# Seven block products for eight in three quarters of a feed-forward matrix

## The chip, the core and the metric

The kernel runs on one core of one Trainium2 chip. A core has five engines with a queue each: TensorE (PE) multiplies matrices, VectorE (DVE) and ScalarE (ACT) work element by element, GpSimd (POOL) here only issues DMAs, and SyncE (SP) issues the DMAs that load weights. Each engine takes its instructions in order; engines wait for each other through semaphores. TensorE reads SBUF and writes PSUM, which has eight banks of 128 x 512 float32; VectorE and ScalarE read both. Sixteen DMA engines serve all queues.

The metric is the time of one execution on the device, in microseconds (us), as the median of several runs.

## The reference

A hybrid encoder block over 256 tokens of width 2048 in float32: gated linear attention beside a Hyena convolution, merged, projected, added to the input and normalised; then a feed-forward part with width 8192. The change is in that last part:

```
    ff = jnp.square(jax.nn.relu(h @ w_ff1[l])) @ w_ff2[l]
    h = _layernorm(DEEPNORM_ALPHA * h + ff, ln2_g[l], ln2_b[l])
```

`h` is 256 x 2048, `w_ff1` 2048 x 8192, `w_ff2` 8192 x 2048.

## The kernel before

**Precision.** Each float32 operand is held as two parts: `hi`, rounded by a copy into TensorE's fast format on ScalarE (line 85), and `lo`, the rest, a subtraction on VectorE (line 86). A product of two operands is then hi x hi + hi x lo + lo x hi. A weight block is 128 x 2048 float32 (1 MB). `fetch` (line 93) loads one into one of three `raw` buffers from SP's queue and splits it in two halves of 1024 columns, each into one of three `whi` and three `wlo` buffers (`weight_half`, line 107).

**First matrix.** A block gives 128 of the 8192 channels for all 256 tokens. `channel_products` (line 140) runs, for each of 16 slices of the input, one matmul of 512 columns (hi weight against hi and lo activation side by side, line 146) and one of 256 (lo weight against hi activation, line 150). `channel_sum` (line 155) adds the two column halves of the result: ScalarE copies one, VectorE adds the other. `channel_pair` (line 161) does two blocks; `ff1` (line 1073) then squares the positive part on VectorE (line 1078) and splits the result into hi and lo.

**Second matrix.** `token_products` (line 194) takes a block that holds four slices of 512 columns: for each slice and each of two token blocks three matmuls of 512 columns (lines 205 to 207), 24 a block. `token_group` (line 209) runs four blocks into one PSUM bank for each token block, and `add_ff` (line 1089) adds the finished 128 x 512 sums to `z1`, the residual, on VectorE.

**Order.** The 8192 channels are done in four quarters of 2048: 16 blocks of the first matrix (`ff1(q)`) and 16 of the second (`ff2(q)`). Lines 1107 to 1117 run ff1(0), ff1(1), ff2(0), ff1(2), ff2(1), ff1(3), ff2(2), ff2(3). Within an engine's queue a scheduler orders instructions from their place in the program and an estimate of when their inputs are ready; `keep_in_program_order` fixes an instruction's place among the others that are fixed, `high_priority` moves it ahead, and `issue_after` ties it behind another instruction.

**Around it.** Before the first quarter, the first layer norm turns `z1` into `hT`, the normalised activations with channels on partitions, by TensorE transposes (line 1017), ScalarE copies and VectorE subtractions (line 86); `begin_three` (line 1038) starts three blocks during that. Four additions of the norm's bias rows to `z1` (line 1084) are tied behind VectorE's square of the blocks 2 to 5 (line 1083). `load_rows` (line 910) loads the second norm's scale and bias rows, from ScalarE's queue, after ff1(0). The last four blocks of the second matrix are held in SBUF (`resident`, line 918), so that the last column group can be finished token block by token block before the second layer norm.

Of the kernel before, what the change touches and what calls it, by code (L numbers as in the profile page):

```python
# [16 lines left out]
P = 128  # L17
# [12 lines left out]
W_OUT_END = 177  # L30
OPENING = 5
# [11 lines left out]
def block_kernel(  # L43
# [117 lines left out]
    def channel_pair(act, name, dst=None, scale=1.0, begun=None):  # L161
        if dst is None:
            dst = base.tile([P, 2, L], F32, tag="sum", name=f"{name}_s")
        for c in range(2):
            if begun:
                ps, parts, n = begun.pop(0)
                finish_block(ps, act, parts, n)
            else:
                ps = channel_psum(f"{name}_{c}")
                parts = next_block()  # L170
                for h in range(2):
                    channel_products(ps, act, parts[h], range(8 * h, 8 * h + 8))
            channel_sum(dst[:, c], ps, f"{name}_l{c}", scale)
            pump()
        return dst
# [742 lines left out]
    def resident(slots):  # L918
        parts = []
        for hi, lo in slots:  # L920
# [4 lines left out]
            for h in range(2):  # L925
                cs = slice(h * 1024, (h + 1) * 1024)
                split_hi_lo(hi[:, cs], lo[:, cs], raw[:, cs])
            parts.append([(hi[:, 0:1024], lo[:, 0:1024]), (hi[:, 1024:], lo[:, 1024:])])
        return parts

# [43 lines left out]
    for i, t in ((0, turn_b), (1, turn_i)):  # L974
        raw = ep.tile([P, 4, P], F32, tag="aff", bufs=1, name=f"turn{i}")
# [19 lines left out]
    stop_at[0] = nblk  # L995
# [40 lines left out]
    fts = {}  # L1036

# [35 lines left out]
    def ff1(qi):  # L1073
        begun = begin_three() if qi == 0 else []
        f = act_tile(ep, "f", f"f{qi}") if qi % 2 == 0 else act_tile(base, "xT", f"f{qi}")
        for c2 in range(8):
            r = channel_pair(hT, f"f{qi}_{c2}", begun=begun)
            sq = nc.vector.scalar_tensor_tensor(r, r, 0.0, r, op0=ALU.max, op1=ALU.mult)
            s = slice(2 * c2, 2 * c2 + 2)
            split_hi_lo(f[:, s, 0], f[:, s, 1], r)  # L1080
            if qi == 0 and 2 <= c2 < 6:
# [3 lines left out]
        fts[qi] = f  # L1085
# [3 lines left out]
    def add_ff(ps, tb, at, n, qi, last=False):  # L1089
        zc = z1[:, tb, at:at + n]  # L1090
        if qi == 0:
            nc.vector.scalar_tensor_tensor(zc, zc, ALPHA, ps, op0=ALU.mult, op1=ALU.add)
        else:
            nc.vector.tensor_tensor(zc, zc, ps, op=ALU.add)
        if qi == QT - 1:
            for i in range(n // 256):
                nc.vector.bn_stats(st2[:, tb, at // 256 + i, :], zc[:, i * 256:(i + 1) * 256])
            if not last:
                nc.vector.tensor_tensor(zc, zc, rows2[:, 0, at:at + n], op=ALU.mult)

    def ff2(qi, groups=4):
        for g in range(groups):
            pss = token_group(fts[qi], f"w2_{qi}{g}")
            for tb in range(NT):
                add_ff(pss[tb], tb, g * 512, 512, qi)
# [12 lines left out]
    minus = ep.tile([P, P], F32, tag="minus", name="minus")  # L1118
    nc.vector.tensor_scalar(minus, ident, -1.0, None, op0=ALU.mult)
    unit = ep.tile([P, P], F32R, tag="unit", name="unit")  # L1120
    nc.scalar.copy(unit, ident)
    zg = tuple(ep.tile([P, D], F32R, tag=t, name=f"{t}_z") for t in ("xh", "xl"))
    for at in (0, 768):
        split_hi_lo(zg[0][:, at:at + 768], zg[1][:, at:at + 768], z1[:, 1, at:at + 768])

    def affine(tb, at, n, rs, nb):
        zc = z1[:, tb, at:at + n]
        t = ep.tile([P, 512], F32, tag="aff", bufs=1, name=f"aff{tb}_{at}")[:, 0:n]
# [7 lines left out]
    token_products([ps], fts[3], parts, [0], 0)  # L1136
    pss = [psum_main(f"w2_33_1{ch}") for ch in range(2)]
    add_ff(ps, 0, 1536, 512, 3)
# [4 lines left out]
    column_products([None, pss], fts[3], parts, [1], 0)  # L1143
    CENTRED = ((0, 512), (512, 512), (1024, 256), (1280, 256))
    po = {}
    for at, n in CENTRED[:3]:
        po[at] = psum_side(f"lo{at}")
        for part in zg:
            tc.keep_in_program_order(MM(po[at], unit, part[:, at:at + 512], start=(part is zg[0]), stop=False))
    po[1280] = po[1024][:, 256:]  # L1150
    add_ff(pss[0][:, 0:256], 1, 1536, 256, 3, last=True)
    late = z1[:, 1, 1536:2048]
    with tc.high_priority(), tc.issue_after(done.ins):
        add_ff(pss[1][:, 0:256], 1, 1792, 256, 3, last=True)
# [21 lines left out]
def _layout(a):  # L1176
# [24 lines left out]
    for i in range(NCH // 2):  # L1201
# [4 lines left out]
    f2q = [tok(w2[D * i:D * (i + 1)]) for i in range(QT)]  # L1206
# [4 lines left out]
        + [f1q[0], f1q[1], f2q[0], f1q[2], f2q[1], f1q[3], f2q[2], f2q[3]], axis=0)  # L1211
# [100 lines left out]
```

## Time and profile before

| | |
|---|---|
| median of 3 runs | 1825.76 us (1825.61 to 1826.41) |
| the profiled execution, first to last instruction (span) | 1826.2 us |
| mean granted TensorE clock in it | 1.000 |
| matmuls of the second matrix, start of the first and of the last | 1288.9 and 1815.7 us after the start |
| HBM read, written | 369.28 MB, 16.25 MB |

Of the profiled execution no other time is known than its span, which lies within the three runs. How to read a profile line: times are in us from the span's start, durations in us unless marked ns; `L205` is a line of the kernel; `w<-whi,f` says that tile `w` is written from `whi` and `f`; `x2` counts instructions; what stands in brackets is the engine's idle time before it and what ended that. PE is TensorE's matmuls, PEld its weight loads, which overlap them. Matmuls are pipelined, so one that is shown with 0.39 us can be followed by the next much sooner.

### The profile page before, as it was taken

How to read it: one execution, taken by the hardware profiler on the slowest of the kernel's cores; microseconds unless marked ns; L12 is line 12 of the kernel's file. 1: busy time of each engine (PE TensorE's matmuls, PEld its weight loads, DVE VectorE, ACT ScalarE, POOL GpSimd, SP SyncE). 2: the span in 40 equal slices, each digit the busy share in tenths (PEclk: the TensorE clock that was granted, in tenths of full speed). 3: DMA queues.
4: the chain of work that ended last, by engine and by line, in shares of the span. 5: the costliest groups of instructions: out<-in, count | busy, mean ns of one | idle time of the engine just before them, and what ended most of it. 6: DMA issues, size and time to landing. Idle time of an engine off the chain costs nothing.

```text
span 1826.2 us, 22887 instructions
## 1 busy us (share of the span) xinstructions
PE 1817.0 (99%) x8931; PEld 1533.8 (84%) x8931; DVE 1286.8 (70%) x1587; ACT 924.1 (51%) x1207; POOL 80.4 (4%) x121
## 2 busy tenths in 40 slices
PE   9999999999999999999999999999999999999998
PEld 7888888888888888888888889888888888888887
DVE  6789887875689899898755567666545655565467
ACT  6678668865444444444544445444434443443332
POOL 1011110000111101020000000000000000000000
PEclk9999999999999999999999999999999999999999
DMA  8668765345788979796544763545554555555453
GB/s 326 222 257 293 253 220 204 141 162 210 235 281 255 320 249 274 259 281 230 215 186 185 288 252 137 210 185 188 193 196 186 193 195 187 195 195 187 188 197 123
DMA packets 65452, 399.55 MB, mean 219 GB/s; under 512 B 8280, under 2 KB 10856, under 8 KB 24640
## 3 DMA queue, kind: packets, MB, share of 16 engines
q1 hardware_dynamic: 47808, 336.61, 49.1%
q0 software_dynamic: 10480, 41.81, 9.9%
q10 hardware_dynamic: 7056, 19.67, 3.0%
q8 instruction: 70, 1.15, 0.2%
q14 instruction: 38, 0.31, 0.0%
HBM read 369.28 MB, written 16.25 MB: 211 GB/s over the span
## 4 chain that ended last, share of the span: by engine, by line
PE 97%; DMA 1%; DVE 1%; ACT 0%; issue 0%; SPq 0%; DVEq 0%; POOL 0%; ACTq 0%
PE f L146 12%; PE f L150 6%; PE w L205 6%; PE w L207 6%; PE w L206 6%; PE g L206 3%; PE g L205 3%; PE g L207 3%; PE ux L207 3%; PE ux L206 3%; PE ux L205 3%; PE k L146 2%; PE v L206 2%; PE v L205 2%; PE v L207 2%; PE go L206 2%
## 5 line engine op out<-in xcount | busy, mean ns | idle before, releaser
L86 DVE TENSOR_TENSOR wlo<-raw,whi 128x1024 fp32r<-128x1024 f32 x584 | 712.3, 1222 | 356.5 <-ACT whi L85 353.4
L85 ACT CAST whi<-raw 128x1024 fp32r<-128x1024 f32 x584 | 614.0, 1053 | 576.1 <-PE w L207 186.5
L146 PE MATMUL f<-hT,whi 128*128 128x512 f32 x984 | 235.1, 391 | 0.0
L146 PEld LDWEIGHTS f<-hT,whi 128*128 128x128 f32 x984 | 180.8, 188 | 35.0
L206 PE MATMUL w<-wlo,f 128*128 128x512 f32 x480 | 186.7, 389 | 0.0
L207 PE MATMUL w<-whi,f 128*128 128x512 f32 x480 | 186.7, 389 | 0.0
L205 PE MATMUL w<-whi,f 128*128 128x512 f32 x480 | 167.4, 389 | 0.0
L150 PEld LDWEIGHTS f<-hT,wlo 128*128 128x128 f32 x984 | 126.2, 191 | 4.8
L150 PE MATMUL f<-hT,wlo 128*128 128x256 f32 x984 | 127.7, 283 | 0.0
L158 ACT ACTIVATE f_l<-f 128x256 f32<-128x256 f32 x64 | 24.6, 384 | 162.2 <-PE f L146 159.3
L207 PEld LDWEIGHTS w<-whi,f 128*128 128x128 f32 x480 | 90.1, 188 | 18.8
L205 PEld LDWEIGHTS w<-whi,f 128*128 128x128 f32 x480 | 90.1, 188 | 18.7
L206 PEld LDWEIGHTS w<-wlo,f 128*128 128x128 f32 x480 | 90.1, 188 | 18.7
L159 DVE SCALAR_TENSOR_TENSOR f_s<-f,f_l 128x256 f32<-128x256 f32 x64 | 27.2, 425 | 105.0 <-ACT f_l L158 105.0
L206 PE MATMUL g<-wlo,xT 128*128 128x512 f32 x256 | 100.1, 391 | 0.0
L207 PE MATMUL ux<-whi,xT 128*128 128x512 f32 x256 | 99.9, 390 | 0.0
L207 PE MATMUL g<-whi,xT 128*128 128x512 f32 x256 | 99.8, 390 | 0.0
L206 PE MATMUL ux<-wlo,xT 128*128 128x512 f32 x256 | 99.6, 389 | 0.0
L205 PE MATMUL g<-whi,xT 128*128 128x512 f32 x256 | 93.8, 392 | 0.0
L205 PE MATMUL ux<-whi,xT 128*128 128x512 f32 x256 | 89.7, 389 | 0.0
L206 PEld LDWEIGHTS g<-wlo,xT 128*128 128x128 f32 x256 | 48.1, 188 | 10.1 <-DVE wlo L86 0.2
L206 PEld LDWEIGHTS ux<-wlo,xT 128*128 128x128 f32 x256 | 48.1, 188 | 10.1
(428 smaller groups left out, 3235.4 us busy)
## 6 DMA issues: line engine op xcount, KB each, us to landing
raw<-wblk SPq DMA_DIRECT2D x300, 1024.0 KB, 4.9
Td<-T POOLq DMA_DIRECT2D x32, 384.0 KB, 5.5
conv_sb<-conv_rows SPq DMA_DIRECT2D x12, 1024.0 KB, 11.7
Tl<-Td POOLq DMA_DIRECT2D x16, 768.0 KB, 9.1
w<-w4s ACTq DMA_DIRECT2D x16, 512.0 KB, 5.7
xw<-first SPq DMA_DIRECT2D x5, 896.0 KB, 13.4
zr<-ln_rows ACTq DMA_DIRECT2D x4, 1024.0 KB, 10.5
cx<-shift POOLq DMA_DIRECT2D x8, 508.0 KB, 8.4
```

The source lines that it names most:

```text
L85: return (nc.scalar.copy(hi, src), nc.vector.tensor_tensor(lo, src, hi.bitcast(F32), op=ALU.subtract))
L86: nc.vector.tensor_tensor(lo, src, hi.bitcast(F32), op=ALU.subtract))
L146: MM(ps[:, :, ts], hi[:, js], act[:, kt, :, ts], start=(kt == 0 and opens), stop=(kt == KT - 1))
L150: MM(ps[:, 0, ts], lo[:, js], act[:, kt, 0, ts], start=False, stop=False)
L158: nc.scalar.activation(low, ps[:, 1], AF.Copy, scale=scale)
L159: nc.vector.scalar_tensor_tensor(dst, ps[:, 0], scale, low, op0=ALU.mult, op1=ALU.add)
L205: MM(pss[tb], sh, wh, start=(kt == 0), stop=False)
L206: MM(pss[tb], sh, wl, start=False, stop=False)
L207: MM(pss[tb], sl, wh, start=False, stop=(kt == KT - 1))
```

## The change

Three quarters of the second matrix are done with seven block products in place of eight (Strassen's scheme, in Winograd's form). A "pair" is 256 rows of the matrix by a group of 1024 columns, seen as 2 x 2 units of 128 x 512. With two token blocks and two row blocks of activations, a plain pair needs 2 x 2 x 2 products of three matmuls each; now seven products run into seven PSUM banks over the eight pairs of a group, three matmuls each, and the results are joined by additions.

- Activations: `forms` makes seven operands out of the four activation quadrants of a pair (three quadrants as they are, four sums) and splits them. Positive part and square are two ScalarE instructions now (`squares`).
- Weights: a pair's four units come in one 1 MB block, `ring_load`, into one of three persistent buffers. `plain_split` splits three units as they are, then replaces unit 0 and unit 3 by sums on VectorE; two DMAs from GpSimd's queue add into unit 1 (512 columns read again from HBM) and into unit 2 (from unit 3, in SBUF), 256 KB each. `pair_split` splits the two VectorE sums, `last_split` the two DMA sums.
- Order: 48 slots (`ff_pairs`), each with one pair of the second matrix and one block of the first for the next quarter (`block_load`, `half_split`). TensorE's part of a slot is, in order: three products on plain units, two on the VectorE sums, the first half of the block, the last two products of the pair before, the second half of the block. Most instructions of the slots are kept in program order on their engines (`pin`).
- Sums: after the eighth pair of a group, `take_sum` takes each bank out to SBUF (on VectorE, in the first quarter four of seven on ScalarE); `join_sums` combines them into `z1`, eight VectorE instructions a group of columns. Four of the seven sums lie where the second norm's rows were, so `load_rows(2)` comes after the joins, early in the last quarter.
- The first quarter's 16 blocks of the first matrix run ahead of the slots (`ff1_first`), the last quarter of the second matrix after them as before, out of the plain activations. `issue_after` for the four bias rows names the square as before, which is a ScalarE instruction now.
- Some tiles share other buffers (`resident_pieces`, `unit`, the turned rows' raw tile, the last group's weights).

```
+FF_PAIRS = W_OUT_END + 16
...
+    FORM = (0, 6, 2, 3, 5, 4, 1)
+    zacc = zr[:, 2:4].rearrange("p a (b c) -> p (a b) c", c=512).rearrange("p (n k) c -> p n k c", n=2)
+    fa = [base.tile([P, 8192], F32R, tag="xT", name="fa0"), None]
+    def fa_slot(i):
+        if fa[1] is None:
+            fa[1] = ep.tile([P, 8192], F32R, tag="f", name="fa1")
+        t = fa[i // 4][:, i % 4 * 1792:(i % 4 + 1) * 1792]
+        return t.rearrange("p (h k j) -> p h k j", h=2, j=P)
...
+    def pin(ins):
+        return tc.keep_in_program_order(ins) if pinned[0] else ins
+    def VT(dst, a, b, op):
+        return pin(nc.vector.tensor_tensor(dst, a, b, op=op))
...
+    def quad_sum(i, c, ps, name):
+        low = base.tile([P, L], F32, tag="low", name=name)
+        dst = quads(i)[:, 2 * c:2 * c + 2][:, ::-1]
+        halves = [a.rearrange("p (t j) -> p t j", j=P) for a in (ps[:, 0], low)]
+        with tc.high_priority():
+            cast(low, ps[:, 1])
+            VT(dst, halves[0], halves[1], ALU.add)
+    def squares(i):
+        q = quads(i)
+        pin(nc.scalar.activation(q, q, AF.Relu))
+        return pin(nc.scalar.activation(q, q, AF.Square))
...
+    def forms(i, plain=False):
+        q, slot = quads(i), fa_slot(i)
+        hi, lo = slot[:, 0], slot[:, 1]
+        if plain:
+            cast(hi[:, 0:4], q)
+            rest(lo[:, 0:4], q, hi[:, 0:4])
+            return
+        t = base.tile([P, 2, P], F32, tag="as", name=f"fw{i}")
+        cast(hi[:, 0:3], q[:, 1:4])
+        VT(t, q[:, 0:1].broadcast_to([P, 2, P]), q[:, 1:3][:, ::-1], ALU.subtract)
+        cast(hi[:, 3:5], t)
+        VT(q[:, 0], q[:, 1], t[:, 0], ALU.subtract)
+        rest(lo[:, 0:3], q[:, 1:4], hi[:, 0:3])
+        VT(q[:, 2], q[:, 3], q[:, 0], ALU.subtract)
+        cast(hi[:, 5:7], q[:, 0:3:2])
+        rest(lo[:, 3:5], t, hi[:, 3:5])
+        rest(lo[:, 5:7], q[:, 0:3:2], hi[:, 5:7])
...
+    def ring_load(p):
+        nc.sync.dma_start(ring_tile(p), wblk[FF_PAIRS + 2 * p])
...
+    def plain_split(p):
+        raw, n = ring_tile(p), FF_PAIRS + 2 * p
+        hi = ep.tile([P, D], F32R, tag="xh", name=f"b_h{p}")
+        lo = ep.tile([P, 1024], F32R, tag="wx", name=f"b_l{p}")
+        u = units(raw)
+        at = slice(0, 1024), slice(1024, 1536)
+        low = lo, hi[:, 1536:2048]
+        for c in at:
+            cast(hi[:, c], raw[:, c])
+        for c, dst in zip(at, low):
+            rest(dst, raw[:, c], hi[:, c])
+        VT(u[0], u[0], u[3], ALU.add)
+        VT(u[3], u[0], u[1], ALU.add)
+        nc.gpsimd.dma_start(u[1], wblk[n, :, 1536:2048], accum_op=ALU.add)
+        nc.gpsimd.dma_start(u[2], u[3], accum_op=ALU.add)
+        h = units(hi)
+        pieces_of[p, 0] = list(zip(h[:3], units(lo) + h[3:]))
...
+    def pair_split(p):
+        hi, lo = weight_half(FF_PAIRS + 2 * p, 0)
+        split_units(p, 1, hi, lo, raw_units(p)[:, 0:4:3])
+    def last_split(p):
+        fa_slot(4)
+        hi, lo = (t[:, 7168:8192] for t in fa)
+        split_units(p, 2, hi, lo, raw_units(p)[:, 1:3])
...
+    def block_load(p):
+        if block_raw[p % 2] is None:
+            block_raw[p % 2] = ep.tile([P, D], F32, tag=("xl", "fraw")[p % 2], name=f"fraw{p}")
+        nc.sync.dma_start(block_raw[p % 2], wblk[FF_PAIRS + 1 + 2 * p])
+    half_parts = {}
+    def half_split(p, h):
+        hi, lo = weight_half(FF_PAIRS + 1 + 2 * p, h)
+        src = block_raw[p % 2][:, h * 1024:(h + 1) * 1024]
+        cast(hi, src)
+        rest(lo, src, hi)
+        half_parts[p, h] = (hi, lo)
+        if h and p + 2 < SLOTS:
+            block_load(p + 2)
...
+            sq = squares(c2)
+            forms(c2)
+            if 2 <= c2 < 6:
                 zc = z1[:, 1, (c2 - 2) * 512:(c2 - 1) * 512]
                 with tc.issue_after(sq.ins):
                     nc.vector.tensor_tensor(zc, zc, rows1[:, 1, (c2 - 2) * 512:(c2 - 1) * 512], op=ALU.add)
...
+    def form_products(pss, p, which, ks):
+        i = p % 8
+        slot = fa_slot(i)
+        for k, (wh, wl) in zip(ks, pieces_of.pop((p, which))):
+            ps, f = pss[k], FORM[k]
+            sh, sl = slot[:, 0, f], slot[:, 1, f]
+            pin(MM(ps, sh, wh, start=(i == 0), stop=False))
+            MM(ps, sh, wl, start=False, stop=False)
+            pin(MM(ps, sl, wh, start=False, stop=(i == 7)))
+        if i == 7:
+            for k in ks:
+                take_sum(p // 16, p // 8 % 2, k, pss[k])
+    def take_sum(q, g, k, ps):
+        c1, c2 = slice(g * 1024, g * 1024 + 512), slice(g * 1024 + 512, g * 1024 + 1024)
+        d = [zacc[:, g, 0], z1[:, 0, c2], z1[:, 0, c1], zacc[:, g, 1], zacc[:, g, 2], zacc[:, g, 3], z1[:, 1, c1]][k]
+        with tc.high_priority():
+            if q == 0 and k in (1, 2, 6):
+                pin(nc.vector.scalar_tensor_tensor(d, d, ALPHA, ps, op0=ALU.mult, op1=ALU.add))
+            elif q == 0:
+                cast(d, ps)
+            else:
+                VT(d, d, ps, ALU.add)
...
+    def join_sums(g):
+        TT = nc.vector.tensor_tensor
+        c1, c2 = slice(g * 1024, g * 1024 + 512), slice(g * 1024 + 512, g * 1024 + 1024)
+        p1, p5, p6, p7 = (zacc[:, g, k] for k in range(4))
+        z11, z12, z21, z22 = z1[:, 0, c1], z1[:, 0, c2], z1[:, 1, c1], z1[:, 1, c2]
+        return [
+            lambda: TT(z11, z11, p1, op=ALU.add),
+            lambda: TT(p6, p6, p1, op=ALU.subtract),
...
+    def ff_pairs():
+        pss = [psum_side(f"w{j}") if j not in (2, 3, 4) else psum_main(f"w{j}") for j in range(7)]
+        joins = []
+        for s in range(SLOTS):
+            more = s + 1 < SLOTS
+            pinned[0] = True
+            form_products(pss, s, 0, (0, 1, 2))
+            if more:
+                plain_split(s + 1)
+            form_products(pss, s, 1, (3, 4))
+            ps = channel_psum(f"f{s // 16 + 1}_{s % 16}")
+            channel_products(ps, hT, half_parts.pop((s, 0)), range(8))
+            if more:
+                half_split(s + 1, 0)
+                pair_split(s + 1)
+            if s:
+                form_products(pss, s - 1, 2, (5, 6))
+                if s == SLOTS - 8:
+                    joins = join_sums(0)
+            last_split(s)
+            if s + 2 < SLOTS:
+                ring_load(s + 2)
+            channel_products(ps, hT, half_parts.pop((s, 1)), range(8, 16))
+            i, c = divmod(s % 16, 2)
+            quad_sum(i, c, ps, f"f{s // 16 + 1}_l{s % 16}")
+            if more:
+                half_split(s + 1, 1)
+            if s >= 9 and (s - 9) % 16 < 8:
+                forms((s - 9) % 16, s >= 2 * 16 + 9)
+            if c:
+                squares(i)
+            if joins:
+                joins.pop(0)()
+            pinned[0] = False
+            if s == SLOTS - 2:
+                stop_at[0] = nblk - 4
+                fetched[0] = FF_PAIRS + 2 * SLOTS
+            for _ in range(max(0, s - SLOTS + 3)):
+                fetch()
+        return pss, joins
+    def ff_close(pss, joins):
+        form_products(pss, SLOTS - 1, 2, (5, 6))
+        forms(7, True)
+        for j in joins + join_sums(1):
+            j()
...
-    ff1(0)
-    rows2 = load_rows(2)
-    ff1(1)
-    ff2(0)
-    ff1(2)
-    ff2(1)
-    ff1(3)
-    ff2(2)
-    stop_at[0] = nblk - 4
-    ff2(3, 3)
-    parts = resident(halves(ep, "f", "wr2") + halves(ep, "hT", "wr3"))
+        nc.vector.tensor_tensor(zc, zc, ps, op=ALU.add)
+        for i in range(n // 256):
+            nc.vector.bn_stats(st2[:, tb, at // 256 + i, :], zc[:, i * 256:(i + 1) * 256])
+        if not last:
+            nc.vector.tensor_tensor(zc, zc, rows2[:, 0, at:at + n], op=ALU.mult)
+    ff1_first()
+    for h in range(2):
+        half_split(0, h)
+    open_sums = ff_pairs()
+    f3 = Quarter()
+    for g in range(3):
+        pss = [psum_main(f"w2_3{g}_{tb}") for tb in range(NT)]
+        for b in range(4):
+            token_products(pss, f3, [next_block()], range(NT), b)
+            if g == b == 0:
+                ff_close(*open_sums)
+                rows2 = load_rows(2)
+        for tb in range(NT):
+            add_ff(pss[tb], tb, g * 512, 512)
...
-    f2q = [tok(w2[D * i:D * (i + 1)]) for i in range(QT)]
+    quad = w2[:3 * D].reshape(3, 8, 2, P, 2, 2, 512)
+    quad = np.stack([quad[:, :, 0, :, :, 0], quad[:, :, 1, :, :, 1], quad[:, :, 1, :, :, 0], quad[:, :, 0, :, :, 1]],
+                    axis=3)
+    quad = quad.transpose(0, 4, 1, 2, 3, 5).reshape(3, 16, P, D)
+    pairs = [np.stack([quad[i], f1q[i + 1]], axis=1).reshape(32, P, D) for i in range(3)]
...
-        + [f1q[0], f1q[1], f2q[0], f1q[2], f2q[1], f1q[3], f2q[2], f2q[3]], axis=0)
+        + [f1q[0]] + pairs + [tok(w2[3 * D:])], axis=0)
```

More of the change, by code (lines that the diff above doesn't have):

```diff
@@ L924, in resident @@
             nc.sync.dma_start(raw, wblk[n])
[L925 to L928, printed above, removed]
-        return parts
+            for h, (hi, lo) in enumerate(part):
+                split_hi_lo(hi, lo, raw[:, h * 1024:(h + 1) * 1024])
+        return parts
+    def resident(slots):
+        return resident_pieces([[(hi[:, c:c + 1024], lo[:, c:c + 1024]) for c in (0, 1024)] for hi, lo in slots])
     def halves(pool, tag, name):
@@ L1087, in block_kernel, with add_ff @@
+    def ff_close(pss, joins):
[3 more added lines that the diff above has]
+            j()
     st2 = ep.tile([P, NT, 8, 6], F32, tag="bst", bufs=2, name="bst2")
-    def add_ff(ps, tb, at, n, qi, last=False):
+    def add_ff(ps, tb, at, n, last=False):
         zc = z1[:, tb, at:at + n]
[L1091 to L1099, printed above, removed]
```

132 lines of the change are left out of this document (88 added, 44 removed).

## The prediction

> **What bounds the kernel now.** I read the page first (busy shares, chain of work that ended last), then what TensorE waited for, then the timelines of the feed-forward stretch.
>
> ```profile
> span 1826.2 us, 22887 instructions
> PE 1817.0 (99%) x8931; PEld 1533.8 (84%) x8931; DVE 1286.8 (70%) x1587; ACT 924.1 (51%) x1207; POOL 80.4 (4%) x121
> PE 97%; DMA 1%; DVE 1%; ACT 0%; issue 0%; SPq 0%; DVEq 0%; POOL 0%; ACTq 0%
> ```
> ```profile
> PE warm L271 <- DVE ones_sb L333: 1.5, 1, 1.5
> PE hb L428 <- ACT T L456: 1.1, 1, 1.1
> PE lo L1169 <- ACT dg L1162: 0.8, 1, 0.8
> PE ht L1017 <- DVE hT L86: 0.6, 1, 0.6
> ```
> TensorE is 97% of the chain, and all its waits together (us in total, times, longest) are 4 us. A matmul left out is time won, as long as no other engine comes up to TensorE's pace; a stall of TensorE is time lost in full. So I need that pace, and the load of the others.
>
> ```profile
> 1500.37 0.62 PE L205 MATMUL w<-whi,f 128*128 128x512 f32 x2
> ...
> 1503.09 0.62 PE L205 MATMUL w<-whi,f 128*128 128x512 f32 x2
> ```
> ```profile
> 1188.90 0.38 ACT L158 ACTIVATE f_l<-f 128x256 f32<-128x256 f32 x1 [2.70 <-PE f L146]
> 1189.18 1.04 ACT L85 CAST whi<-raw 128x1024 fp32r<-128x1024 f32 x1
> 1190.50 0.62 ACT L85 CAST f<-f_s 128x512 fp32r<-128x512 f32 x1 [0.28 <-DVE f_s L1078]
> 1191.03 1.05 ACT L85 CAST whi<-raw 128x1024 fp32r<-128x1024 f32 x1
> ...
> 1200.03 0.38 ACT L158 ACTIVATE f_l<-f 128x256 f32<-128x256 f32 x1 [2.70 <-PE f L146]
> ```
> Columns: start, duration, instruction. Half a block of the second matrix (2 x 2 x 3 = 12 matmuls of 512 columns) comes round in 1503.09 - 1500.37 = 2.72 us: 0.2267 us each. Two blocks of the first matrix, counted at their column sums on ScalarE, take 1200.03 - 1188.90 = 11.13, so 5.56 us each.
>
> **Removed.** Three quarters of the second matrix have 3 x 384 = 1152 matmuls; seven products for eight leave 1008. 144 x 0.2267 = **32.6 us** come off TensorE.
>
> **The new slot.** In each of 48 slots TensorE does one pair of the second matrix (21 matmuls, 4.76) and one block of the first (5.56): 10.33 us. In program order: A, three products, to 2.04; B, two products, to 3.40; C, first half of the block, to 6.18; D, the last two products of the pair before, to 7.54; E, second half, to 10.33. The queues of VectorE and ScalarE follow a written order, so their work in each slot decides, not their average:
>
> ```profile
> 1350.00:1450.00 100.00, 100.00 (x540) 86.83 (x539) 58.81 (x66) 44.59 (x55) 0.00 (x0) 1.00 0.51 194
> ```
> (Stretch, then busy PE, PEld, DVE, ACT, POOL; granted clock, DMA share, GB/s.) VectorE is at 59% before. Its prices are distances from start to start, because its instructions overlap too:
>
> ```profile
> 1101.28 0.42 DVE L951 TENSOR_TENSOR zr<-zr 128x256 f32<-128x256 f32 x1
> 1101.62 0.42 DVE L953 TENSOR_TENSOR zr<-zr 128x256 f32<-128x256 f32 x1
> ...
> 1189.32 0.42 DVE L159 SCALAR_TENSOR_TENSOR f_s<-f,f_l 128x256 f32<-128x256 f32 x1 [1.86 <-ACT f_l L158]
> 1189.78 0.69 DVE L1078 SCALAR_TENSOR_TENSOR f_s<-f_s 128x512 f32<-128x512 f32 x1
> 1190.39 1.22 DVE L86 TENSOR_TENSOR wlo<-raw,whi 128x1024 fp32r<-128x1024 f32 x1
> 1191.52 0.68 DVE L86 TENSOR_TENSOR f<-f_s,f 128x512 fp32r<-128x512 f32 x1
> 1192.12 1.22 DVE L86 TENSOR_TENSOR wlo<-raw,whi 128x1024 fp32r<-128x1024 f32 x1
> ...
> 1508.24 1.28 DVE L1094 TENSOR_TENSOR zr<-zr,w 128x512 f32<-128x512 f32 x2
> ```
> 1.14 us for 1024 columns (1190.39 to 1191.52), 0.60 for 512 (also out of PSUM: 1.28 - 0.68), 0.34 for 256; by the same slope 0.47 for 384 and 0.21 for 128. An instruction that needs the result of the one before (1189.78) starts 0.04 after its end: 0.46 after a 256, 0.73 after a 512. ScalarE likewise: a 256 is followed after 0.28, a 512 after 0.53, and a cast of 1024 is finished after 1.05.
>
> A plain slot on VectorE: five splits of 1024 columns 5.70, one of 512 0.60, two weight sums, the second needing the first, 0.73 + 0.60, the block's sum 0.34: **8.0 us**, covered by 10.33. ScalarE has five casts of 1024, one of 512, the 256 and, every other slot, two of 512: about 6, covered. Within the slot: ScalarE's first cast follows A, so VectorE's splits start at 3.2 and the second weight sum ends at 6.3; the split of the block's first half waits for C (cast to 7.3) and ends at 8.4; the split of the summed pair ends at 9.6. TensorE needs that for the next B, at 10.33 + 2.04 = 12.4. Reserve: 2.8 us.
>
> Slots 9 to 16 and 25 to 32 also build the seven activation forms: on VectorE 0.45 + 0.21 + 0.47 + 0.21 + 0.34 + 0.2 (waiting for ScalarE's last form cast) + 0.34 = 2.25. ScalarE can cast the next pair (1.05) only after that last form cast, and VectorE, whose next instruction is that pair's split, stands 0.6; in every other slot the relu and the square (0.66 + 0.53) come in between, and it stands 1.8. So 10.85 and 12.03 us, mean 11.44: **1.11 over TensorE's 10.33**, 17.8 over 16 slots. Taking sums out of PSUM adds instructions of 0.60: 2 + 1 at slots 15 and 16, 5 + 2 at 31 and 32, 6.0 us. Less the reserve, twice 2.8, TensorE stands **18.2 us**, in front of B. Bounds: 0, if the standing is filled after all; and 0.5 us more a slot for handoffs that no row shows, 8 more.
>
> The first quarter builds its forms too, but there two blocks (11.13) need 4 x 1.14 + 2 x 0.34 + 2.25 = 7.5 of VectorE: 0, at most 1 where the first pair's splits come in.
>
> **The DMAs that add.** No row shows 256 KB added from HBM, or two such in a row. The nearest are the convolution's 508 KB adding DMAs on the same queue (KB, median us from issue to landing), with POOL's issue times (ns):
>
> ```profile
> cx<-shift POOLq DMA_DIRECT2D x8, 508.0 KB, 8.4
> ...
> cv<-shift POOLq DMA_DIRECT2D x4, 508.0 KB, 10.9
> ```
> ```profile
> L742 POOL DMA_DIRECT2D cx<-shift x16: 758/862/1160, 492.9 to 820.3; - x16
> ```
> ```profile
> 812.00:816.00 4.00, 4.00 (x21) 3.32 (x20) 2.14 (x3) 2.61 (x4) 0.00 (x0) 1.00 0.98 96
> ```
> ```profile
> raw<-wblk SPq DMA_DIRECT2D x300, 1024.0 KB, 4.9
> ```
> POOL is idle in this stretch, and issuing costs it 0.76 to 1.16 us; the two together are 512 KB. The window is nearly all an adding DMA: 0.98 share at 96 GB/s, so 512 KB is up to 5.4 us of all engines. The two plain blocks of a slot are 0.51 x 11.1 = 5.7. Bound from above 11.1 of a 10.33 us slot; from below, if added bytes cost what plain ones do, 7.1. The landing is needed when ScalarE casts the last pair, one slot later at 18.6 (behind the half and the pair cast): 12.3 us after the second sum at 6.3. I take 10, between the rows: hidden, price 0. Behind that cast stand E's column sum and the next half's cast, so the next C and E would be late next. The plain blocks land in 4.9 and are issued 11 us ahead of use or more, when the last split of the slot before is done: 0.
>
> **Moved.** The four row additions after the first layer norm hung on a VectorE square. The square is on ScalarE now, and in the built order of VectorE the four stand among the last subtractions of the normalised activations:
>
> ```profile
> 1113.45 0.75 DVE L86 TENSOR_TENSOR hT<-ht,hT 128x256 fp32r<-128x256 f32 x2
> 1114.55 2.04 DVE L86 TENSOR_TENSOR hT<-ht,hT 128x512 fp32r<-128x512 f32 x3 [0.34 <-ACT hT L85]
> ```
> ```profile
> 1115.24 4.31 PE f L179 x36
> ```
> The subtractions end at 1116.59. TensorE starts on their results at 1115.24 and needs the last four column blocks 12 matmuls of 0.12 later, at 1116.7. Four times 0.60 in front, less the gap of 0.34: **+2.1** (0 to 2.4).
>
> At the close, VectorE takes five sums out of PSUM behind two splits, and the last quarter's first matmul needs the third one's bank: two splits end at 9.5 in the slot, three sums at 11.4, TensorE is there at 10.33: **+1.1** (0 to 2). The 16 joins (9.6 us) spread over blocks in which VectorE has 2 x 1.14 of 5.44 to do: 0. The second norm's rows can load only after the joins, about 16 us into the last quarter, and are used at 27:
>
> ```profile
> zr<-ln_rows ACTq DMA_DIRECT2D x4, 1024.0 KB, 10.5
> ```
> Just hidden, by two blocks of matmuls: 0; VectorE's next split has 1.8 us to spare if not.
>
> **Sum.** 1826.2 - 32.6 + 18.2 + 2.1 + 1.1 = 1815.0. The span lies within the runs (1825.61 to 1826.41), 0.4 over their median: **1815 us**.
>
> **A rule against it.** The Trainium skill (VectorE: DVE Perf Modes, "The DRAIN you can't avoid") says that the next operation does not start before the pipe is empty. By it every instruction of the slot costs its whole duration, and the sum is rival 3's 1836. The trace disagrees: the instruction at 1191.52 starts 0.09 before the one at 1190.39 ends.
>
> **Rivals.**
> 1. *All covered* (18%): VectorE's standing overlaps with something, and the forms fit. For it: 59% share before. Against: the fixed order, 5.6 us of reserve for 23.8 of excess. 1815 - 18.2 = 1797.
> 2. *Adds land too late* (25%), the one that ends slower. Place: ScalarE's cast of the last pair. From 12.3 us of landing on, a loop (second sum, DMAs, this cast, ScalarE's queue, next cast, second sum) that runs over two slots sets the pace: each further us costs half a us in each of 48 slots, 24 us. Level with before at 12.7; at 14 it is 1815 + 41 = 1856. For it: 10.9 among other traffic, a source in HBM, DMA near full. Against: 8.4, and the shares added up only from above.
> 3. *VectorE does not overlap here* (10%): nearly all its instructions wait for ScalarE, so each of the 16 in a form slot costs 0.08 more (1.22 - 1.14), 1.3 us in 16 slots: 1815 + 21 = 1836. Against: the split at 1190.39 waits for a cast too, and starts 0.08 before its predecessor ends.
>
> **How the numbers follow.** The forecast has 47%, by its bounds 1797 to 1824. 0.2% (3.65 us) is about what a measurement of this kernel can tell from no change. Faster: 37 of its 47, rival 1's 18, 4 of rival 2: 0.59. Same: 8, 3 and 1 of rival 3: 0.12. Slower: 2, 18 and 9: 0.29. The range goes from just under rival 1, 1795, past rival 3 to 1840 (a landing of 13.3), and leaves out later adds.
>
> **What would show it.** Right: 144 matmuls fewer at 0.2267; TensorE waiting for the pair's split from about slots 12 and 28 on, 0.5 to 1.7 us a slot and up to 3 at the sums, and hardly elsewhere; VectorE over 90% there, near 80% in plain slots. Wrong: ScalarE's last-pair cast waiting for DMA in every slot (rival 2); no waits in form slots (rival 1); a granted clock under 1.00 around the waits, or another spacing of the matmuls, which would take from the 32.6 itself.

## The result, and the profile after

| kernel | median us (lowest to highest) | ratio to before, 95% interval |
|---|---|---|
| before, same runs | 1825.97 (1825.61 to 1826.41) | |
| changed | 1817.89 (1817.21 to 1818.74) | 0.9955 (0.9941 to 0.9969) |

The forecast was 1815, so the time came out 2.9 us later: 8.1 us gained of the 32.6 that the matmuls left out are worth. The profiled execution of the changed kernel took 1818.21 us, 1.8 more than its span.

From the page of the changed kernel (span; busy time, share and count of each engine; shares of the chain that ended last):

```profile
span 1816.4 us, 23481 instructions
PE 1797.7 (99%) x8787; PEld 1505.1 (83%) x8787; DVE 1454.9 (80%) x1893; ACT 1042.5 (57%) x1423; POOL 164.8 (9%) x217
PE 87%; DVE 7%; ACT 3%; issue 3%; DMA 1%; ACTq 0%; DVEq 0%; POOL 0%
```

8931 - 8787 = 144 matmuls fewer, as counted. TensorE is still nearly always busy by the page, but its share of the chain falls from 97% to 87%: VectorE and ScalarE take 9 of these 10, "issue" (time in which an engine waited for nothing that the profile shows) the rest. What TensorE waited for (us in total, times, longest):

```profile
PE w L1245 <- DVE wlo L1101: 6.6, 8, 1.8
PE f L147 <- DVE fr L1101: 1.9, 2, 1.2
PE w L1244 <- ACT whi L1104: 1.0, 5, 0.2
```

The first line is the second matmul of B, which waits for the split of the two weight sums on VectorE: the place that the prediction named. The second line the prediction did not have: seven of the eight banks hold the sums of the seven products, and twice a block's first matmul waits until VectorE has added up the block before and so freed the eighth. The view counts only what is left of a gap after the modelled end of the matmul before, and misses most of it. The length of the slots shows all. Once in a slot, at its end, ScalarE copies half of the block's column sum (start, duration, instruction):

```profile
1218.90 0.37 ACT L1104 COPY f_l<-f 128x256 f32<-128x256 f32 x1 [1.47 <-PE f L147]
...
1301.68 0.37 ACT L1104 COPY f_l<-f 128x256 f32<-128x256 f32 x1 [1.75 <-PE f L147]
1313.47 0.37 ACT L1104 COPY f_l<-f 128x256 f32<-128x256 f32 x1
1324.52 0.36 ACT L1104 COPY f_l<-f 128x256 f32<-128x256 f32 x1
1336.72 0.37 ACT L1104 COPY f_l<-f 128x256 f32<-128x256 f32 x1
1347.76 0.36 ACT L1104 COPY f_l<-f 128x256 f32<-128x256 f32 x1
...
1717.61 0.37 ACT L1104 COPY f_l<-f 128x256 f32<-128x256 f32 x1 [1.74 <-PE f L147]
```

The eight plain slots from slot 1's copy to slot 9's take 1301.68 - 1218.90 = 82.78, 10.35 each. Then form slots alternate: 11.05, 12.20, 11.04. (The forms of a slot are built after its copy, so "odd form slot" below means the time from an odd slot's copy to the next one, as from slot 11's at 1324.52 to slot 12's at 1336.72. In these slots ScalarE reaches the copy later than TensorE is done; the copies at 1301.68 and 1717.61 waited for TensorE, and between them the lags cancel.) From the end of slot 9 to the end of slot 47 there are 38 slots in 415.93 us; at 10.35 they would take 393.2. So the slots hold **22.7 us of stalls** (18.2 predicted), all in slots 10 to 18, 26 to 34 and, 0.5 us, 40 to 43. VectorE in a plain stretch and in one of form slots (stretch, its length, busy PE, PEld, DVE, ACT, POOL, clock, DMA share, GB/s):

```profile
1211.00:1310.00 99.00, 99.00 (x512) 84.88 (x511) 81.18 (x94) 63.43 (x83) 15.83 (x18) 1.00 0.88 263
1313.00:1395.00 82.00, 77.45 (x375) 61.19 (x374) 73.34 (x109) 53.47 (x81) 12.21 (x15) 1.00 0.76 225
```

82% and 89% (near 80 and over 90 were predicted): what is missing to 100% in the second is VectorE standing. The timeline of VectorE and of ScalarE in one odd form slot shows where:

```profile
1329.45 0.42 DVE L1101 TENSOR_TENSOR fa<-fr,fa 128x256 fp32r<-128x256 f32 x1
1331.58 1.23 DVE L1101 TENSOR_TENSOR b_l<-ring,b_h 128x1024 fp32r<-128x1024 f32 x1 [1.71 <-ACT b_h L1104]
```
```profile
1329.01 0.41 ACT L1104 CAST fa<-fr 128x256 fp32r<-128x256 f32 x1 [0.71 <-DVE fr L1101]
1329.32 0.63 ACT L1119 ACTIVATE fr<-fr 128x512 f32<-128x512 f32 x1
1329.98 0.63 ACT L1120 ACTIVATE fr<-fr 128x512 f32<-128x512 f32 x1
1330.52 1.55 ACT L1104 CAST b_h<-ring 128x1024 fp32r<-128x1024 f32 x2
```

VectorE has done its last form at 1329.87 and stands 1.71 us, because ScalarE does a relu and a square ahead of the next pair's cast. In an even slot those two are missing and the same wait is 0.53:

```profile
1319.37 1.22 DVE L1101 TENSOR_TENSOR b_l<-ring,b_h 128x1024 fp32r<-128x1024 f32 x1 [0.53 <-ACT b_h L1104]
```

### The profile page after: what moved, and what is told of

It reads as the page before. It is cut to its first block, busy times and chain, and to the rows that moved or that the text cites. A ratio compares the mean times of both kernels' runs of the same rounds, so it can differ in the third digit from the quotient of the medians.

```text
span 1816.4 us, 23481 instructions
## 1 busy us (share of the span) xinstructions
PE 1797.7 (99%) x8787; PEld 1505.1 (83%) x8787; DVE 1454.9 (80%) x1893; ACT 1042.5 (57%) x1423; POOL 164.8 (9%) x217
## 3 DMA queue, kind: packets, MB, share of 16 engines
q0 software_dynamic: 24304, 66.99, 18.2%
## 4 chain that ended last, share of the span: by engine, by line
PE 87%; DVE 7%; ACT 3%; issue 3%; DMA 1%; ACTq 0%; DVEq 0%; POOL 0%
PE f L147 9%; PE f L151 5%; PE g L200 3%; PE g L199 3%; PE g L201 3%; PE ux L199 3%; PE ux L200 3%; PE ux L201 3%; PE w L1245 3%; PE w L1244 3%; PE w L1246 3%; PE k L147 2%; PE v L201 2%; PE v L200 2%; PE v L199 2%
## 5 line engine op out<-in xcount | busy, mean ns | idle before, releaser
L86 ACT CAST whi<-raw 128x1024 fp32r<-128x1024 f32 x392 | 412.7, 1055 | 408.6 <-PE ux L201 84.4
L87 DVE TENSOR_TENSOR wlo<-raw,whi 128x1024 fp32r<-128x1024 f32 x392 | 477.1, 1221 | 206.8 <-ACT whi L86 205.5
L1101 DVE TENSOR_TENSOR wlo<-fraw,whi 128x1024 fp32r<-128x1024 f32 x96 | 117.0, 1219 | 11.8 <-ACT whi L1104 11.8
L1104 ACT CAST whi<-ring 128x1024 fp32r<-128x1024 f32 x48 | 50.6, 1054 | 90.6 <-DVE ring L1101 83.8
L1104 ACT CAST whi<-fraw 128x1024 fp32r<-128x1024 f32 x96 | 100.7, 1049 | 0.2 <-PE f L147 0.2
L1101 DVE TENSOR_TENSOR b_l<-ring,b_h 128x1024 fp32r<-128x1024 f32 x48 | 58.7, 1224 | 33.1 <-ACT b_h L1104 33.0
L1104 ACT CAST b_h<-ring 128x1024 fp32r<-128x1024 f32 x96 | 74.9, 829 | 8.8 <-ACT whi L1104 8.2
L1101 DVE TENSOR_TENSOR ring<-ring 128x512 f32<-128x512 f32 x96 | 66.0, 688 | 1.6
L1101 DVE TENSOR_TENSOR wlo<-ring,whi 128x1024 fp32r<-128x1024 f32 x48 | 58.8, 1225 | 2.7 <-ACT whi L1104 1.2
L1101 DVE TENSOR_TENSOR fa<-ring,fa 128x1024 fp32r<-128x1024 f32 x48 | 58.5, 1219 | 0.8 <-ACT fa L1104 0.8
## 6 DMA issues: line engine op xcount, KB each, us to landing
conv_sb<-conv_rows SPq DMA_DIRECT2D x12, 1024.0 KB, 11.5
```

Of the source, the lines that this page charges most:

```text
L86: return (nc.scalar.copy(hi, src), nc.vector.tensor_tensor(lo, src, hi.bitcast(F32), op=ALU.subtract))
L87: nc.vector.tensor_tensor(lo, src, hi.bitcast(F32), op=ALU.subtract))
L1101: return pin(nc.vector.tensor_tensor(dst, a, b, op=op))
L1104: return pin(nc.scalar.copy(hi, src))
```

## The experiments

All are edits of the changed kernel. Their times, with the kernel before at 1826.56 to 1826.70 in the same runs. The changed kernel was not run beside them, and the kernel before lay 0.6 to 0.7 us over its 1825.97, so differences to 1817.89 are good to about that, and smaller ones are read from the traces.

| run | median us | ratio to before, 95% interval |
|---|---|---|
| squares later | 1808.1 | 0.9899 (0.9885 to 0.9914) |
| forms in two | 1797.57 | 0.984 (0.9824 to 0.9857) |
| forms cast only | 1795.34 | 0.983 (0.9815 to 0.9845) |
| one add on VectorE | 1830.09 | 1.002 (1.001 to 1.0029) |
| adds in a row | 1865.36, one run | |
| three in a row | 1925.62, one run | |
| forms off the sums' slots | 1796.13 | 0.9834 (0.9817 to 0.985) |
| rows later | 1795.95 | 0.9833 (0.9818 to 0.9848) |
| plain copies | 1818.84, one run | |

**Squares later.** Is the standing what makes the odd form slots long?

```
             form_products(pss, s, 1, (3, 4))
             ...
+            if s and s % 2 == 0:
+                squares((s - 1) % 16 // 2)
             if more:
                 half_split(s + 1, 0)
...
-            if c:
+            if s == SLOTS - 1:
                 squares(i)
```

> The relu and the square of a finished pair move on ScalarE from the end of an odd slot to the middle of the next one, behind the casts of the next pair and ahead of the cast of the block's first half. Theory (VectorE stands because ScalarE reaches the next pair's cast late): an odd form slot gets as short as an even one, 12.2 to 11.04 us, eight times: 1817.9 - 9.4 = 1808.5 us; even form slots stay at 11.04. Rival (VectorE's own work sets the form slots, the standing is filled by something else): 1818 us. Rival (the moved pair of instructions makes the cast of the block's first half late): no shorter slots, stalls at the first half of the block, 1818 or more.

1808.1 us. Odd form slots took 11.03 to 11.04 us like the even ones. No work was taken away; two ScalarE instructions of 0.63 us moved to where ScalarE waits 1.8 us for the weight sum anyway. That 9.8 us came back (9.6 between the copies of slots 9 and 47) shows that ScalarE's order, not VectorE's work alone, made these slots.

**Forms in two**, on top of the later squares. The rest of the standing, 0.53 a slot, is a handoff: the last cast of a form waits for VectorE, and the next pair's cast waits behind it.

```
         cast(hi[:, 0:3], q[:, 1:4])
         VT(t, q[:, 0:1].broadcast_to([P, 2, P]), q[:, 1:3][:, ::-1], ALU.subtract)
-        cast(hi[:, 3:5], t)
         VT(q[:, 0], q[:, 1], t[:, 0], ALU.subtract)
         rest(lo[:, 0:3], q[:, 1:4], hi[:, 0:3])
         VT(q[:, 2], q[:, 3], q[:, 0], ALU.subtract)
-        cast(hi[:, 5:7], q[:, 0:3:2])
-        rest(lo[:, 3:5], t, hi[:, 3:5])
-        rest(lo[:, 5:7], q[:, 0:3:2], hi[:, 5:7])
+        def second():
+            cast(hi[:, 3:5], t)
+            cast(hi[:, 5:7], q[:, 0:3:2])
+            rest(lo[:, 3:5], t, hi[:, 3:5])
+            rest(lo[:, 5:7], q[:, 0:3:2], hi[:, 5:7])
...
                 plain_split(s + 1)
+            if second_half:
+                second_half.pop()()
             form_products(pss, s, 1, (3, 4))
```

> As the run with the later squares, and the forms are cut in two: the casts and subtractions of the two pairs of summed operands come one slot later, behind the next pair's casts (ScalarE) and weight sums (VectorE), so that no cast of the next pair waits for a form. Same work. Theory: VectorE then has 8.0 + 2.25 + 0.1 = 10.3 us in a form slot against TensorE's 10.33, and hardly stands; the 22.8 us of stalls in the slots fall to what the sums out of PSUM cost beyond the reserve, 0 to 3: 1795 to 1798 us. Rival (handoffs between the two engines cost about 0.5 us a slot wherever they stand): 16 x 0.5 more, 1804. Rival (the standing is not what the stalls are made of): 1808 to 1818.

1797.57 us, inside the theory's 1795 to 1798. VectorE's timeline has no wait left between the forms and the next pair's split:

```profile
1303.19 1.23 DVE L1101 TENSOR_TENSOR wlo<-fraw,whi 128x1024 fp32r<-128x1024 f32 x1 [0.52 <-ACT whi L1104]
...
1305.58 0.29 DVE L1101 TENSOR_TENSOR fr<-fr 128x128 f32<-128x128 f32 x1
1305.79 1.22 DVE L1101 TENSOR_TENSOR b_l<-ring,b_h 128x1024 fp32r<-128x1024 f32 x1
...
1313.48 1.22 DVE L1101 TENSOR_TENSOR wlo<-fraw,whi 128x1024 fp32r<-128x1024 f32 x1
```

One round from 1303.19 to 1313.48 is 10.29 us with all the form work in it: at TensorE's pace. The next pair's split now starts 0.21 after the last activation sum. Of the 2.3 us of stalls that remain, 2.0 lie in slots 31 to 34, where VectorE also takes sums out of PSUM.

**Forms cast only.** How much is left if VectorE has no form work at all?

```
+        if pinned[0]:
+            cast(hi[:, 0:3], q[:, 1:4])
+            cast(hi[:, 3:5], q[:, 0:2])
+            cast(hi[:, 5:7], q[:, 0:3:2])
+            return
```

> Leaves out, in the slots, the four activation sums and the seven low parts of the forms (VectorE's part of them), and keeps ScalarE's casts, relu and square. Theory (VectorE's form work and the standing it brings are the stalls): no form slot above 10.4 us, all of 22.8 gone but the sums out of PSUM: 1795 to 1797 us. Rival (ScalarE's casts and squares in front of the next pair's cast are enough to stall): odd slots stay 0.5 to 1.2 us long, 1800 to 1805. Rival (the stalls come from elsewhere, DMA or the weights' buffers): 1815 or more.

1795.34 us, with no slot up to 39 above 10.40, although the relu and the square still stand ahead of the next pair's cast. Leaving out all of VectorE's form work gains only 2.2 us more than putting it in a better order.

**One add on VectorE.** What is 0.6 us of VectorE worth in plain and in form slots?

```
-        nc.gpsimd.dma_start(u[2], u[3], accum_op=ALU.add)
+        VT(u[2], u[2], u[3], ALU.add)
```

> One of the two DMAs that add (unit 3 into unit 2) is a VectorE addition of 512 columns, right behind the second weight sum. Theory (plain slots have 2.3 us of VectorE to spare, form slots none): plain slots unchanged at 10.34, the 16 form slots 0.48 to 0.73 us longer each, 7.7 to 11.7 us: 1825.6 to 1829.6 us. Rival (VectorE sets the pace of every slot): 48 x 0.6, 1847. Rival (there is room in VectorE's waits): 1818.

1830.09 us, slower than before the change and 0.5 over the top of what was expected. Plain slots stayed at 10.29 to 10.40 but for slot 25 (10.92); form slots went from 11.04 and 12.21 to 11.63 and 12.82, 0.60 each, 9.6 over 16. Of the other 2.6 us, 1.8 lie in slots 40 to 43 (43.7 us there in place of 41.9); the rest was not taken apart. A third weight sum on VectorE would have turned the change into a loss, for the sake of 16 slots of 48.

**Adds in a row.** How close is the landing of the adding DMAs to being late?

```
-        nc.gpsimd.dma_start(u[2], u[3], accum_op=ALU.add)
+        nc.gpsimd.dma_start(u[2], u[1], accum_op=ALU.add)
```

> Against the changed kernel (1817.9 us): the second of the two DMAs that add takes its source from the unit that the first one writes, and so has to wait for the first one's landing (unit 2 gets other numbers). Bytes, sizes and queue are the same; only the landing of a pair's last sum moves from about 7 us after VectorE's second sum to 10 to 12 (0.5 to the issue, 4.3, 5.0, and up to 2 of issuing). Theory (nothing needs it before 12.3 us): no change, 1817 to 1819 us, no wait of ScalarE's last-pair cast for DMA. Rival (the landing already decides, at some point below 12.3): each us beyond that point costs about 24 us, 1830 or more.

1865.36 us: my expectation failed, by its landing. In the changed kernel the two DMAs land (KB, us from issue)

```profile
ring<-wblk POOLq DMA_DIRECT2D x48, 256.0 KB, 4.3
ring<-ring POOLq DMA_DIRECT2D x48, 256.0 KB, 5.0
```

and in a row

```profile
ring<-wblk POOLq DMA_DIRECT2D x48, 256.0 KB, 4.7
ring<-ring POOLq DMA_DIRECT2D x48, 256.0 KB, 8.5
```

The second, issued 5 us later, took 8.5 and not 5.0 us; it then runs beside the next blocks' loads, which is a likely reason but was not tested by itself. VectorE's sums of this kernel (two in a row) and ScalarE's cast that waits for them:

```profile
1249.12 1.41 DVE L1101 TENSOR_TENSOR ring<-ring 128x512 f32<-128x512 f32 x2
...
1272.11 1.41 DVE L1101 TENSOR_TENSOR ring<-ring 128x512 f32<-128x512 f32 x2
```
```profile
1265.43 1.05 ACT L1104 CAST fa<-ring 128x1024 fp32r<-128x1024 f32 x1 [5.55 <-DMA ring<-ring]
```

From the end of the second sum (1249.12 + 1.41 = 1250.53) to the cast are 14.9 us, over the 12.3 of the prediction's rival 2; from the cast to the next second sum's end (1273.52) 8.1. The loop over two slots is 23.0 us, and that is its pace: 11.5 a slot here. Over all slots in which this cast waits for the DMA, the median from second sum to cast is 14.8 us. By rival 2's price (24 us for each us over 12.3) the time says 12.3 + 47.5 / 24 = 14.3.

**Three in a row.**

```
-        nc.gpsimd.dma_start(u[2], u[3], accum_op=ALU.add)
+        nc.gpsimd.dma_start(u[2][:, 0:256], u[1][:, 0:256], accum_op=ALU.add)
+        nc.gpsimd.dma_start(u[2][:, 256:], u[2][:, 0:256], accum_op=ALU.add)
```

> As the run with the two adding DMAs in a row, and the second is cut in two of 128 KB, the later of which takes its source from the earlier one: a chain of three, with the same bytes, that lands about 14 to 16 us after the second sum. Theory (the loop over two slots of the prediction: level up to 12.3 us, then half a us in each of 48 slots for each us): (14 to 16 - 12.3) x 24 = 41 to 89 us more than 1818, 1859 to 1907, with ScalarE's last-pair cast waiting for DMA in every slot. Rival (a late sum delays only the last two products, which wait in TensorE's queue once, and the later slots follow at the old pace): 1820 to 1823. Rival (hidden whatever it is): 1818.

1925.62 us, 107.7 over the changed kernel, more than the 89 expected; by the same price a landing of 16.8. Measured as above, the median is 16.9. The later landing has a second cause, on GpSimd's queue:

```profile
1257.63 0.86 POOL L1171 DMA_DIRECT2D ring<-ring  x1 [5.61 <-DMA ring<-ring]
1258.16 1.22 POOL L1169 DMA_DIRECT2D ring<-wblk  x1
```

VectorE's second sum for the next pair ended at 1256.71, but its first DMA stands behind the third DMA of the pair before and is issued 1.5 us later. Both runs show the place of rival 2, and that the change itself stays clear of it. They bear out its price only roughly: 14.8 and 16.9 would have cost 60 and 110 us at 24 each, and 47.5 and 107.7 were measured, in one run each. The mean granted clock of the second was 0.981 (0.999 in the changed kernel); what that adds was not taken apart.

**Plain copies.** What does the adding itself cost?

```
-        nc.gpsimd.dma_start(u[1], wblk[n, :, 1536:2048], accum_op=ALU.add)
-        nc.gpsimd.dma_start(u[2], u[3], accum_op=ALU.add)
+        nc.gpsimd.dma_start(u[1], wblk[n, :, 1536:2048])
+        nc.gpsimd.dma_start(u[2], u[3])
```

> Against the changed kernel (1817.9 us): the two DMAs of a pair that add copy instead (same sources, targets, bytes and order; units 1 and 2 get other numbers). In the changed kernel's plain slots their queue takes 31.4% of the DMA engines, 3.25 us of a 10.34 us slot for 512 KB. Theory (an added byte costs the DMA engines more than a copied one, and neither decides the time): the queue's share falls to about half, 1.4 us a slot by the plain blocks' 5.7 us for 2048 KB, landings get shorter than 4.3 and 5.0 us, and the time stays at 1817 to 1819 us with the same stalls in the form slots. Rival (the adding DMAs slow the block loads and so the slots): 1810 or less.

1818.84 us with the same stalls; the copies land 3.6 and 3.7 us after their issue, not 4.3 and 5.0. Over six plain slots (62 us) the queue's part of the DMA engines (packets, MB, share), first of the changed kernel:

```profile
q0 software_dynamic: 1752, 3.19, 31.4%
```

and with copies:

```profile
q0 software_dynamic: 961, 3.15, 15.1%
```

The adding doubles what a byte costs the DMA engines, 3.25 for 1.56 us a slot, and none of it reaches the time.

**Forms off the sums' slots**, on top of the forms in two, and **rows later**, on top of both:

```
+            at = {9: 0, 10: 1, 11: 2, 12: 3, 13: 4, 14: 5, 17: 6, 19: 7}
...
+            elif s - s // 25 * 16 in at:
+                forms(at[s - s // 25 * 16])
```

> As the run with the forms in two, and in the second and third quarter the last two forms of each quarter come two slots apart, after the slots in which VectorE takes the sums out of PSUM (slots 17 and 19, 33 and 35 in place of 15, 16, 31, 32). Same work. Theory (what is left of the stalls, 2.0 us at slots 31 to 34, is VectorE doing sums and forms in the same slots): no slot above 10.45 but those that catch up, 1797.6 - 2.0 = 1795.5 us. Rival (the sums alone stall TensorE): 1797.5.

1796.13 us; in the trace the stalls of slots 31 to 34 fall from 2.0 to 1.1 us, half of what was expected. The medians are 1.4 apart and their runs overlap, so the trace carries this, not the time.

```
-            sq = squares(c2)
-            forms(c2)
+            squares(c2)
+            last = forms(c2)
...
-                with tc.issue_after(sq.ins):
+                with tc.issue_after(last.ins):
```

> As the run with the forms off the sums' slots, and the four additions of the first norm's bias rows are tied behind the last instruction of the forms of pairs 2 to 5 on VectorE, so that they leave the chain of the first layer norm. The prediction put them at 2.1 us: 1795.5 - 2.1 = 1793.4. By the trace of the changed kernel (from the first transposes to the end of the first quarter it is 0.5 us longer than before): 1795.0 us, which only the trace can show: the first block's column sum 0.5 us earlier after the last matmul of the projection.

1795.95 us: no difference in the time, 0.54 in the trace. From the first transpose of the first layer norm to the first block's column sum, in the kernel before, the changed kernel and this one:

```profile
1104.46 0.38 PE L1017 MATMUL ht<-ident,zr 128*128 128x128 f32 x2
1121.51 0.38 ACT L158 ACTIVATE f_l<-f 128x256 f32<-128x256 f32 x1 [0.87 <-PE f L184]
```
```profile
1103.43 0.38 PE L1011 MATMUL ht<-ident,zr 128*128 128x128 f32 x2
1121.01 0.38 ACT L1104 COPY f_l<-f 128x256 f32<-128x256 f32 x1 [0.87 <-PE f L178]
```
```profile
1103.10 0.38 PE L1011 MATMUL ht<-ident,zr 128*128 128x128 f32 x2
1120.14 0.37 ACT L1104 COPY f_l<-f 128x256 f32<-128x256 f32 x1 [0.87 <-PE f L178]
```

17.05, 17.58 and 17.04 us. This last kernel, which the time cannot tell from the one before it, beats the changed one by 1.2% and the kernel before the change by 1.7%, with the changed kernel's arithmetic. 1826.6 - 32.6 = 1794.0 would be the end of what the 144 matmuls can give.

## Why the prediction was right, and where it was off

| step | predicted us | measured us |
|---|---|---|
| matmuls left out | -32.6 | -32.6 |
| pace of a plain slot, 10.33 | 0 | +1.0 (10.35, 48 times) |
| stalls in the slots, predicted in front of B | +18.2 | +22.7 |
| four row additions in the first layer norm | +2.1 | +0.5 |
| close | +1.1 | 0 |
| adding DMAs, joins, second norm's rows, first quarter | 0 | 0 |
| sum | -11.2 | -8.4 |

The medians say -8.1. (The spans say -9.8, of which 1.0 had arisen before the first layer norm's transposes, 1104.46 to 1103.43; five of these kernels that are alike up to there reach it between 1102.50 and 1104.02, so this is the scatter of one execution.) The sum started from the span of before as if it were its time. In every later run of the kernel before the time is about 1.8 us longer than the span (1826.70 and 1824.9, for one). By that its profiled execution, with a span of 1826.2, took an estimated 1828.0, some 2 us more than the median. The two errors cancelled, by luck. Why a plain slot takes 10.35 and not 10.33, no run shows.

**Stalls: the mechanism held, the size was 4.5 us short.** A form slot was put at 10.85 and 12.03 and took 11.04 and 12.21. The working missed two small waits of VectorE, seen here in the form slot from 1313.47 on:

```profile
1317.06 0.55 DVE L1101 TENSOR_TENSOR fa<-fr,fa 128x384 fp32r<-128x384 f32 x1
1317.64 0.29 DVE L1101 TENSOR_TENSOR fr<-fr 128x128 f32<-128x128 f32 x1
...
1322.44 1.22 DVE L1101 TENSOR_TENSOR wlo<-fraw,whi 128x1024 fp32r<-128x1024 f32 x1
1323.70 1.23 DVE L1101 TENSOR_TENSOR wlo<-ring,whi 128x1024 fp32r<-128x1024 f32 x1
1324.84 1.22 DVE L1101 TENSOR_TENSOR fa<-ring,fa 128x1024 fp32r<-128x1024 f32 x1
```

The sum at 1317.64 writes a quadrant that the split before it reads, and starts 0.58 after it, not 0.47; the split of the summed pair starts 1.26 after the one before, not 1.14, since ScalarE's cast of it ends only then. Over TensorE's 10.35 that makes 8 x 0.69 + 8 x 1.86 = 20.4 in the form slots, where the prediction had 17.8. (Its terms of the form work add up to 2.22, not 2.25, half a us less over 16 slots.) The sums out of PSUM add 1.8 and 4.2, as predicted (0.60 each). Against these 12.0 and 14.4 us the two groups of slots lost 9.9 and 12.5, so the reserve counted for 2.0 each time and not 2.8, 1.6 in all. The trace of the first group shows why. In slot 9 the split of the summed pair ends 3.7 us ahead of its need (1298.78 + 1.23 = 1300.01, against B's matmul at 1303.69), more than the prediction's reserve. But in the first form slot VectorE still begins with the waits of a plain one (0.90 and 0.53), and from that split to the next, at 1312.66, it takes 13.88 us, where the later odd form slots take 12.21; 3.7 - 1.7 = 2.0. The last 0.5 are the slots 40 to 43, where the prediction had none; 2.6, 1.6 and 0.5 are the 4.5 but for rounding.

**Row additions: the wrong consumer.** The subtractions did end 2.1 us later against the first transpose, as predicted (14.2 us after it, 12.1 before). But TensorE needed the last of them later than the 1116.7 that the prediction gave. It lost 0.5, at the last transposes, which wait 0.34 us for a bank:

```profile
1113.87 0.63 PE L1011 MATMUL ht<-ident,zr 128*128 128x128 f32 x4 [0.34 <-DVE hT L87]
```

**Close.** TensorE was to stand for the third bank. The built order put 24 matmuls of the last quarter in between:

```profile
1717.41 0.61 PE L1244 MATMUL w<-fa,fa 128*128 128x512 f32 x2
1717.86 0.39 PE L199 MATMUL w<-whi,fa 128*128 128x512 f32 x1
...
1723.30 0.39 PE L1245 MATMUL w<-fa 128*128 128x512 f32 x1
```

(1723.30 - 1717.86) / 24 = 0.2267: no gap. The two overestimates, 2.7 us, took back half of the 5.5 that the slots were too cheap, and so the total lay 2.9 from the forecast and the steps up to 4.5. The place and the kind of the stalls were foreseen; that the total came this close is in part luck.

**The rivals.** *All covered* fell for this kernel, and is what the better order reaches: 1796 to 1798 against the 1797 worked out for it. *Adds too late* fell because the landing is 4.3 and 5.0 after the issue, 6 to 7 us after the second sum and not the 10 assumed; the two runs in a row show its place and, roughly, its price. The DMA share, 0.88 x 10.35 = 9.1 us a slot, lies between the bounds 7.1 and 11.1. *VectorE does not overlap* fell: in a saturated slot the instructions at 1323.70 and 1324.84 start 1.14 apart and last 1.23. By the Trainium skill's rule (VectorE: DVE Perf Modes, "The DRAIN you can't avoid") they would be at least 1.23 apart; the trace disagrees, also where VectorE sets the pace. The same section adds that a next operation that is not held starts earlier, and that is what these do.

## What to carry to other kernels

Where two engines feed each other in a fixed order, add up the standing separately from the work: here 16 slots exceeded the pace through the order of a few ScalarE instructions (relu, square and the last casts of the forms), and moving them and the subtractions behind them gave 20 us without taking any work away. Before work is cut from an engine that seems full, look at what the engine that feeds it does between the last instruction and the next one it needs. And for work moved to a DMA, ask how far its landing is from its use, not how many bytes it moves: twice the DMA time per byte cost nothing, while a landing 8 us later cost 47.

## What the hardware showed that was not expected

After a short stall TensorE's clock was lower for some us. In slot 32 of the changed kernel TensorE ran one matmul between 1546.49 and 1549.18 and then this (eight matmuls each):

```profile
1550.66 3.45 PE L147 MATMUL f<-hT,whi 128*128 128x512 f32 x8
...
1557.25 2.00 PE L147 MATMUL f<-hT,whi 128*128 128x512 f32 x8
```

with these granted clocks (third number from the end) in stretches of 2 us:

```profile
1550.00:1552.00 2.00, 2.00 (x6) 1.34 (x5) 2.00 (x4) 0.00 (x0) 0.00 (x0) 0.55 0.83 147
1552.00:1554.00 2.00, 2.00 (x7) 1.53 (x6) 1.79 (x6) 1.20 (x3) 0.00 (x0) 0.60 0.96 406
1554.00:1556.00 2.00, 2.00 (x14) 1.82 (x13) 0.29 (x2) 1.97 (x4) 0.00 (x0) 1.00 0.83 291
```

The Trainium skill (TensorE: Matmul & The Clock Gate, "Part 1: The HAM clock gate") has a clock that is halved after an idle window of about 3.4 us and stays so for about as long. The trace agrees in level and length: 0.55 and 0.60 are 1.7 us lost in 4, as 3.4 us at half clock would be. It differs in what came before: some 2.5 us of standing, with a matmul in between, were enough. The kernel before, which has no such stall, has no stretch of 2 us under 0.97. The lower clock cost nothing in this place: the run with the later squares, which has no such stretch in the slots, has this slot shorter (13.28 to 12.11) by the same 1.17 us as the other odd form slots, so VectorE set the pace.
